# A two-layer encoder trunk on one core: work moved to GpSimd, and the first input ahead of the weights

## The chip, the cores and the metric

The kernel runs on one core of a Trainium2 chip. A core has five engines that run their own instruction streams and meet through semaphores: TensorE (PE in the profile; its weight loads are PEld), VectorE (DVE), ScalarE (ACT), GpSimd (POOL) and SyncE (SP), which here issues all DMAs. The metric is the device time of one execution in microseconds (us); three runs of the kernel before gave 2092.22, 2092.9 and 2097.98, a median of 2092.9.

## The reference

Two request groups, "prompt" (p, 1024 tokens) and "sample" (s, 512 tokens), go through the same two layers of width 1024. Cut to what matters:

```python
for l in range(2):
    z = rmsnorm(h, norm_g[l]) @ w_in[l]                 # 1024 -> 3328, split into 11 parts
    o = concat(hgrn2(...), rglru(...), diff_attn(...))  # three bidirectional branches, 1024 wide
    h = h + o @ w_out[l]
    h = h + sigmoid(h @ ple_gate_w[l]) * (p[l] @ ple_w[l])
y = rmsnorm(h, final_norm)
```

HGRN2 is a gated linear recurrence in chunks of 64, RG-LRU a convolution of width 4 with two scans per channel, and the attention subtracts two softmaxes. All of it is float32.

## The kernel before, in words

Activations lie transposed, 128 channels by 512 tokens in a tile, so the prompt has two token blocks and the sample one. Float32 products are made of three matmuls in a rounded format: every operand is split into a high part (ScalarE rounds it) and a low part (the value less its high part), and TensorE adds high·high, low·high and high·low. `load_split` (line 350) does this for a weight: one DMA of 256 KB into `wr`, a cast to `wh` on ScalarE (line 359) and a subtraction into `wl` on VectorE (line 360). `hilo` (line 326) does it for activations; `proj` (line 364) issues the three times four matmuls of each half of a weight column, 24 for a column of 1024 inputs.

A layer of a group has an input stage A (`phase_a`: projections by `w_in`, then attention, RG-LRU and HGRN2) and an output stage B (`phase_b`, one per token block). B multiplies by the eight columns of `w_out` (line 1067, each evacuated into `bh` on line 1073 and split again), then by the eight of `w_gate` (lines 1078 and 1087) and of the small `w_ple`. Three blocks in two layers make 48 columns of each, and 96 splits of `w_out` and 96 of `w_gate` weights.

The start is `first_norm` for the two prompt blocks: a DMA of each of the eight tiles `x`, a square on ScalarE (line 1135), and four matmuls by a column of ones that sum it (tile `ov`). Then `norm_in` (line 475) spreads 1/rms over the tile `rb`, and for each `x` VectorE multiplies by gain and `rb` (line 487) and `hilo` splits the product.

The order of all instructions is made ahead by a list scheduler in the kernel (`Recorder`). Each operation has a cost and a priority: its place in the program, plus `BIAS` of its stage, minus a share of the rank; offsets move loads forward (`WOFF`) or evacuations (`EVAC`, the lines inside `hp(EVAC)`). The scheduler keeps each engine's list in time by these costs and writes out one fixed sequence per engine. Stage names read A or B, the layer and the group: "A0s" is the sample's input stage in layer 0, with "at", "lru" or "hg" behind it for a branch. The prompt's stage B is woven into the sample's stage A, so that TensorE has matmuls while the branches run. Within an engine the sequence is strict: an instruction that waits holds all behind it.

Of the kernel before, what the change touches and what calls it, by code (L numbers as in the profile page):

```python
# [10 lines left out]
F32 = mybir.dt.float32  # L11
# [19 lines left out]
ORD_S = "aAbBhHlL"  # L31
BUFS = {"act": 32, "wr": 4, "wh": 5, "wl": 4, "pr": 1, "ph": 1, "pl": 1, "ev": 2, "io": 3, "acc": 1, "rb": 1, "tiny": 16, "sm": 4, "pre": 1, "lpr": 1,
        "m2x": 9, "m4x": 9, "m2y": 8, "m4y": 6}
WOFF, EVAC = 400, 900
RANK = 0.55
BIAS = {"A0sat": 400, "A1p": 100, "A1phg": 200, "A1plru": -50, "A1sat": -100, "A1shg": 50, "B0p0": -400, "B0p1": 300, "B0s0": -350, "B1p0": -50, "B1p1": 100, "B1s0": -200}
BANKS = {"pj": 3, "pt": 2, "ov": 1}
LANE = {
# [206 lines left out]
def tile_trunk(ctx: ExitStack, tc: tile.TileContext, a, groups, depth):  # L245
    nc = tc.nc
# [100 lines left out]
            V(8, lambda: nc.vector.scalar_tensor_tensor(out=t[:, c], in0=t[:, c], scalar=-0.5, in1=v[:, c], op0=MUL, op1=MUL), [t, v], [t])  # L347
            V(8, lambda s=s: nc.vector.scalar_tensor_tensor(out=dst[:, c], in0=t[:, c], scalar=1.5, in1=s(), op0=ADD, op1=MUL), [t, sk], [dst])

    def load_split(src, k, c=128, p="w", off=0):  # L350

        w = min(512, k * c)
        kk = w // c
        out = []
        for i in range(k // kk):
            raw, hi, lo = (T(p + x, [128, w], F32 if x == "r" else F32R, p + x) for x in "rhl")
            o = off - WOFF
            DMA(lambda raw=raw, i=i: nc.sync.dma_start(raw.t.rearrange("p (k c) -> p k c", k=kk), src[:, i * kk : i * kk + kk]), [], [raw], 512 * w, off=o, occ=0.4)
            A(w, lambda raw=raw, hi=hi: nc.scalar.copy(hi.t, raw.t), [raw], [hi], off=o)  # L359
            V(w, lambda raw=raw, hi=hi, lo=lo: nc.vector.tensor_tensor(out=lo.t, in0=raw.t, in1=hi.t.bitcast(F32), op=SUB), [raw, hi], [lo], off=o)  # L360
            out.append((hi, lo))
        return out

# [107 lines left out]
    def act(name="act"):  # L471
        return T("act", [128, 512], F32R, name)

    def norm_in(h_src, hkey, rs, gcol, gk, xs, hs=None):
        R.stage = f"norm{gk}"
        with hp(2000):
            pp = bcast_rs(rs, PT())
            pb = W5("rb", name="rb")
            A(512, lambda: nc.scalar.copy(pb.t, pp.t), [pp], [pb])
        for k in range(8):  # L480
            if hs is None:
                h = W5("io", name="nh")
                DMA(lambda h=h, k=k: nc.sync.dma_start(h.t, h_src(k)), [hkey(k)], [h], B2)
            else:
                h = hs[k]
            with hp(2000):
                V(512, lambda h=h, k=k: nc.vector.scalar_tensor_tensor(out=h.t, in0=h.t, scalar=gcol[:, k : k + 1], in1=pb.t, op0=MUL, op1=MUL), [h, pb, gk], [h], ps_=0.06)
                xh, xl = act(), act()
                hilo(h, xh, xl)
            xs[k] = (xh, xl)  # L490

    def head_tail(tg, ro, o, gcol, dk, sg_src, sgk, out_dst, outk, add=None):
# [551 lines left out]
    def phase_b(l, g, tb, n, oT, h_src, hk, hD):  # L1044
# [19 lines left out]
        h1D = dram.tile([8, 128, 512], F32, name=f"h1_{l}_{g}_{tb}")  # L1064
        hs = []
        for m in range(8):
            w = load_split(a["w_out"][l, m], 8)
            p = PJ()
            proj([p], w, [os_])
            h1 = W5("io", name="bh")  # L1070
            DMA(lambda h1=h1, m=m: nc.sync.dma_start(h1.t, h_src(m)), [hk(m)], [h1], B2)
            with hp(EVAC):
                V(512, lambda h1=h1, p=p: nc.vector.tensor_tensor(out=h1.t, in0=p.t, in1=h1.t, op=ADD), [p, h1], [h1])
                DMA(lambda h1=h1, m=m: nc.sync.dma_start(h1D[m], h1.t), [h1], [("h1", l, g, tb, m)], B2)
                xh, xl = act(), act()
                hilo(h1, xh, xl)
            hs.append((xh, xl))
        ahead = [load_split(a["w_gate"][l, m], 8) for m in range(2)]
        for k in range(2):
            xh, xl = act(), act()  # L1080
            r = W5("wr", name="p")
# [2 lines left out]
            ps_.append((xh, xl))  # L1084
        acc = W5("acc", name="acc")
        for m in range(8):
            w = ahead[m] if m < 2 else load_split(a["w_gate"][l, m], 8)
            wpl = load_split(a["w_ple"][l, m], 2, p="p")
            pg = PJ()
            proj([pg], w, [hs])  # L1090
            pp = PJ()
            proj([pp], wpl, [ps_])
            h1 = T("act", [128, 512], F32, "h2") if last else W5("io", name="bh1")
            fin.append(h1)
            DMA(lambda h1=h1, m=m: nc.sync.dma_start(h1.t, h1D[m]), [("h1", l, g, tb, m)], [h1], B2)
            with hp(EVAC):
                th = W5()
                A(512, lambda th=th, pg=pg: nc.scalar.activation(out=th.t, in_=pg.t, func=AF.Tanh, scale=0.5), [pg], [th])
                V(512, lambda th=th, pp=pp: nc.vector.scalar_tensor_tensor(out=th.t, in0=th.t, scalar=1.0, in1=pp.t, op0=ADD, op1=MUL), [th, pp], [th])
                V(512, lambda th=th, h1=h1: nc.vector.scalar_tensor_tensor(out=h1.t, in0=th.t, scalar=0.5, in1=h1.t, op0=MUL, op1=ADD), [th, h1], [h1])  # L1100
                if not last:
                    DMA(lambda h1=h1, m=m: nc.sync.dma_start(hD[m, :, sl], h1.t), [h1], [("h", l, g, tb, m)], B2)
                if m == 0:
                    A(512, lambda h1=h1: nc.scalar.activation(out=acc.t, in_=h1.t, func=AF.Square), [h1], [acc])
                else:
                    sq = W5()
                    A(512, lambda sq=sq, h1=h1: nc.scalar.activation(out=sq.t, in_=h1.t, func=AF.Square), [h1], [sq])
                    V(512, lambda sq=sq: nc.vector.tensor_tensor(out=acc.t, in0=acc.t, in1=sq.t, op=ADD), [acc, sq], [acc])
# [11 lines left out]
    rsd = {}  # L1120
    xs = {g: [[None] * 8 for _ in range(n // 512)] for g, n in groups}

    def first_norm(g, tb, tg="io", by_pe=True):

        hs = []
        rs = T("sm", [128, 4], F32, "rs")
        p = PT("ov") if by_pe else None
        acc = None if by_pe else W5("acc", name="acc")
        for k in range(8):
            x = W5(tg, name="x")  # L1130
            sq = acc if not by_pe and k == 0 else W5()
            DMA(lambda x=x, k=k: nc.sync.dma_start(x.t, a["x_" + g][k, :, blk(tb)]), [], [x], B2)
            hs.append(x)
            with hp(2000):
                A(512, lambda x=x, sq=sq: nc.scalar.activation(out=sq.t, in_=x.t, func=AF.Square), [x], [sq])

                def f(k=k, sq=sq):
                    for t in range(4):
                        mm(p[:, t : t + 1], sq[:, t * 128 : (t + 1) * 128], ones, k == 0 and t == 0, k == 7)

                if by_pe:
                    PE(0.9, f, [sq, "ones"], [p])
                elif k:
                    V(512, lambda sq=sq: nc.vector.tensor_tensor(out=acc.t, in0=acc.t, in1=sq.t, op=ADD), [acc, sq], [acc])
        if by_pe:
            with hp(2000):
                rsqrt(rs, lambda: p[:, 0:4], 4, 1.0 / 1024, EPS, srck=p)
        else:
            rs = stats_rs(acc)
        rsd[g, tb] = rs  # L1150
        return hs

    ng = [lay[l]["vec"][:, V_NG : V_NG + 8] for l in range(depth)]
    (g0, n0), rest = groups[0], groups[1:]
    x0 = first_norm(g0, 0, "m2x")
# [122 lines left out]
```

## Time and profile before

| | |
|---|---|
| median of three runs | 2092.9 us (2092.22 to 2097.98) |
| the profiled execution, its own time | 2098.01 us |
| its span, first to last instruction | 2096.2 us |
| TensorE busy | 1983.0 us, 95% |
| VectorE busy | 1535.0 us, 73% |
| ScalarE busy | 1214.7 us, 58% |
| GpSimd busy | 0.2 us, four memsets |
| granted clock of TensorE, mean | 0.975 |

Busy times are averages over stages with different limits, so they are read by stretch. A busy TensorE is not one at its peak, since the ends of matmuls are modelled; the count of matmuls in a stretch says more. "Idle before" in a row is what an engine waited before that row, with the releaser behind the arrow. PEclk is the granted clock: 1.00 is 2.4 GHz and 0.5 is 1.2 GHz. Layer 0 has its stage A of the prompt up to about 500 us, the sample's stage A with the prompt's stage B from there to about 900, and what is left of stage B up to 1050; layer 1 repeats it.

### The profile page before, as it was taken

The page shows a single profiled execution, that of the slowest core. Times are in us where ns is not written, and L with a number is a line of the kernel's source. Part 1 is how long each engine was busy: PE and PEld are TensorE (multiplying, and loading weights), DVE is VectorE, ACT ScalarE, POOL GpSimd, SP SyncE. Part 2 cuts the span into 40 slices and gives each one's busy share as a digit, 9 for nine tenths or more (in the row PEclk, how much of TensorE's full clock was granted, in tenths as well). Part 3 has the DMA queues.
Part 4 walks back from the last instruction along what each step waited for, and adds up shares of the span by engine and source line. Part 5 has one row for each costly group of instructions (what it writes and reads, how often), then busy time and mean ns, then how long its engine had stood idle before and what let it go on. Part 6 is the DMA issues. An engine that isn't in the chain of part 4 may idle for free.

```text
span 2096.2 us, 38258 instructions
## 1 busy us (share of the span) xinstructions
PE 1983.0 (95%) x14528; PEld 1613.2 (77%) x14528; DVE 1535.0 (73%) x2928; ACT 1214.7 (58%) x2053; POOL 0.2 (0%) x4
## 2 busy tenths in 40 slices
PE   7999889999999999899979988999999999889997
PEld 7887778887878787678767777888788878667875
DVE  5427678888988997754566767787789998785464
ACT  4338795766445468743438766676545654774332
POOL 0000000000000000000000000000000000000000
PEclk9999999999999999999989989999999999989998
DMA  4336433345444455564643462242464354547462
GB/s 154 109 98 195 164 109 110 111 147 167 152 152 149 150 179 186 179 204 161 197 158 127 150 183 86 91 123 85 150 213 146 123 171 158 179 143 258 126 205 89
DMA packets 187575, 316.53 MB, mean 151 GB/s; under 512 B 22016, under 2 KB 43008, under 8 KB 187392
## 3 DMA queue, kind: packets, MB, share of 16 engines
q1 hardware_dynamic: 187392, 314.09, 46.9%
q8 instruction: 115, 1.88, 0.4%
q14 instruction: 68, 0.56, 0.1%
HBM read 229.07 MB, written 84.93 MB: 150 GB/s over the span
## 4 chain that ended last, share of the span: by engine, by line
PE 70%; ACT 12%; DMA 7%; DVE 7%; issue 3%; SPq 0%; DVEq 0%; ACTq 0%
PE pj L316 52%; PE big L316 7%; PE ov L316 5%; PE pt L685 3%; DMA qk_p<-ev 3%; ACT ti L759 2%; ACT tr L759 1%; PE pt L316 1%; ACT T L761 1%; DMA qk_s<-ev 1%; ACT pp L670 1%; ACT tr L763 1%; ACT wh L359 1%; ACT L767 1%; DVE nm L667 1%
## 5 line engine op out<-in xcount | busy, mean ns | idle before, releaser
L316 PE MATMUL pj<-act,wh 128*128 128x512 f32 x3648 | 951.3, 399 | 16.9 <-ACT act L327 9.9
L316 PEld LDWEIGHTS pj<-act,wh 128*128 128x128 f32 x3648 | 683.5, 191 | 173.5 <-ACT act L327 13.9
L316 PE MATMUL pj<-act,wl 128*128 128x512 f32 x1824 | 496.4, 402 | 13.2 <-DVE wl L360 13.2
L316 PEld LDWEIGHTS pj<-act,wl 128*128 128x128 f32 x1824 | 344.3, 192 | 92.8 <-DVE wl L360 16.6
L360 DVE TENSOR_TENSOR wl<-wr,wh 128x512 fp32r<-128x512 f32 x400 | 272.6, 687 | 164.2 <-PE pj L316 111.7
L359 ACT CAST wh<-wr 128x512 fp32r<-128x512 f32 x400 | 243.4, 620 | 241.9 <-PE pj L316 163.7
L670 ACT ACTIVATE pp<-big,nm 128x1024 f32<-128x1024 f32 (+1 forms) x192 | 187.5, 977 | 92.1 <-DVE nm L667 74.4
L667 DVE TENSOR_REDUCE nm<-big 128x1 f32<-128x1024 f32 (+1 forms) x192 | 198.3, 1037 | 10.6 <-PE big L316 10.3
L316 PE MATMUL pj<-wh,act 128*128 128x256 f32 x768 | 146.3, 290 | 2.4 <-DVE ev L548 1.2
L316 PEld LDWEIGHTS pj<-wh,act 128*128 128x128 f32 x768 | 123.4, 194 | 9.3 <-issue 1.9
L316 PE MATMUL big<-ks,qs 96*128 96x512 f32 x320 | 113.5, 430 | 10.5 <-ACT pp L670 6.7
L688 ACT COPY wt<-pt 128x512 f32<-128x512 f32 x160 | 92.2, 588 | 44.1 <-PE pt L685 40.8
L316 PE MATMUL pj<-wl,act 128*128 128x256 f32 x384 | 109.3, 285 | 1.3 <-DVE wl L360 1.3
L677 DVE SCALAR_TENSOR_TENSOR pp<-pp,cc 128x1024 f32<-128x1024 f32 (+1 forms) x96 | 105.9, 1103 | 1.2
L685 PE MATMUL pt<-ident,pp 128*128 128x128 f32 x640 | 95.0, 278 | 2.2 <-DVE ev L591 0.7
L685 PEld LDWEIGHTS pt<-ident,pp 128*128 128x128 f32 x640 | 74.3, 141 | 22.9 <-issue 4.8
L316 PE MATMUL ov<-wt,dv 128*64 128x128 f32 x1280 | 82.2, 280 | 2.8 <-ACT wt L688 2.8
L316 PEld LDWEIGHTS ov<-wt,dv 128*64 128x64 f32 x1280 | 70.4, 139 | 17.0 <-issue 11.9
L759 ACT ACTIVATE tr<-big,der 64x512 f32<-64x512 f32 x96 | 65.4, 681 | 19.3 <-PE big L316 18.2
L316 PEld LDWEIGHTS pj<-wl,act 128*128 128x128 f32 x384 | 74.3, 194 | 1.5 <-DVE wl L360 1.5
L316 PE MATMUL pj<-act,ph 128*128 128x512 f32 x192 | 62.4, 406 | 11.1 <-ACT act L327 9.7
L316 PEld LDWEIGHTS big<-ks,qs 96*128 96x128 f32 x320 | 53.4, 191 | 24.1 <-ACT pp L670 12.3
(188 smaller groups left out, 2390.6 us busy)
## 6 DMA issues: line engine op xcount, KB each, us to landing
wr<-in_w_in SPq DMA_DIRECT2D x176, 256.0 KB
wr<-in_w_out SPq DMA_DIRECT2D x96, 256.0 KB
wr<-in_w_gate SPq DMA_DIRECT2D x96, 256.0 KB
h_p<-bh SPq DMA_DIRECT2D x48, 256.0 KB
sg_p<-ev SPq DMA_DIRECT2D x32, 256.0 KB
wr<-in_w_v SPq DMA_DIRECT2D x32, 256.0 KB
qk_p<-ev SPq DMA_DIRECT2D x32, 256.0 KB
act<-oT_p SPq DMA_DIRECT2D x32, 256.0 KB
```

Of the source, the lines that this page charges most:

```text
L316: nc.tensor.matmul(out, lhsT, rhs, start=start, stop=stop, skip_group_check=True)
L359: A(w, lambda raw=raw, hi=hi: nc.scalar.copy(hi.t, raw.t), [raw], [hi], off=o)
L360: V(w, lambda raw=raw, hi=hi, lo=lo: nc.vector.tensor_tensor(out=lo.t, in0=raw.t, in1=hi.t.bitcast(F32), op=SUB), [raw, hi], [lo], off=o)
L667: V(n, lambda nm=nm, pv=pv: nc.vector.tensor_reduce(out=nm.t, in_=pv(), axis=mybir.AxisListType.X, op=ALU.max, negate=True), [b], [nm])
L670: A(n, lambda p=p, pv=pv, nm=nm, s1=s1, s2=s2, j=j, qt=qt, H=H: nc.scalar.activation(out=p.t, in_=pv(), func=AF.Exp, bias=nm.t, accum_out= ...
L677: V(n, lambda P=P, c=c: nc.vector.scalar_tensor_tensor(out=P[0].t, in0=P[1].t, scalar=c.t, in1=P[0].t, op0=MUL, op1=ADD), [P[0], P[1], c], ...
L685: nc.tensor.transpose(pt[:, kt * 128 : kt * 128 + 128], P[0][:, c0 : c0 + 128], ident)
L688: A(512, lambda wt=wt, pt=pt, kb=kb: nc.scalar.copy(wt[:, blk(kb)], pt.t), [pt], [(wt, kb)])
L759: A(512, lambda dst=dst, pg=pg, r=r, dr=dr, hb=hb, col=col, h=h, o=o: nc.scalar.activation(out=dst[h, dr, :], in_=pg[o, r, :], func=AF.Tan ...
L761: A(512, lambda T2=T2, tr=tr, dr=dr, col=col: nc.scalar.activation(out=T2[:, dr, :], in_=tr[:, dr, :], func=AF.Tanh, scale=d["n2"][:, col] ...
L763: A(512, lambda tr=tr, dr=dr, col=col: nc.scalar.activation(out=tr[:, dr, :], in_=tr[:, dr, :], func=AF.Exp, scale=d["n4"][:, col], bias=d ...
L767: A(1024, lambda T2=T2: nc.scalar.activation(out=T2.t, in_=T2.t, func=AF.Sqrt, scale=-0.25), [(T2, 0), (T2, 1)], [(T2, 0), (T2, 1)], tab=" ...
```

## The change

The low parts of the `w_out` and `w_gate` weights go from VectorE to GpSimd (192 subtractions). In the two first norms, every other tile is multiplied by `rb` on GpSimd; the gain then comes in as the scale of ScalarE's cast and as the scalar of VectorE's subtraction, so that VectorE has one operation for such a tile and not two. The loads of the first eight `x` tiles get an offset of -1500. `EVAC` and seven entries of `BIAS` change, of which two are new.

```diff
-WOFF, EVAC = 400, 900
+WOFF, EVAC = 400, 1100
-BIAS = {"A0sat": 400, "A1p": 100, ... "A1sat": -100, ... "B0p0": -400, ... "B0s0": -350, "B1p0": -50, ... "B1s0": -200}
+BIAS = {"A0sat": 400, "A0shg": -50, ... "A1sat": -150, "A1slru": 200, "B0p0": -200, ... "B0s0": -550, "B1p0": -100, ... "B1s0": -300}
-    def load_split(src, k, c=128, p="w", off=0):
+    def load_split(src, k, c=128, p="w", off=0, pool=False):
...
+            if pool:
+                R("POOL", 1.1, lambda raw=raw, hi=hi, lo=lo: nc.gpsimd.tensor_tensor(out=lo.t, in0=raw.t, in1=hi.t.bitcast(F32), op=SUB), [raw, hi], [lo], lat=1.3, off=o)
+            else:
+                V(w, lambda raw=raw, hi=hi, lo=lo: nc.vector.tensor_tensor(out=lo.t, in0=raw.t, in1=hi.t.bitcast(F32), op=SUB), [raw, hi], [lo], off=o)
...
+                if hs is not None and k % 2:
+                    R("POOL", 1.1, lambda h=h: nc.gpsimd.tensor_tensor(out=h.t, in0=h.t, in1=pb.t, op=MUL), [h, pb], [h], lat=1.3)
+                    A(512, lambda h=h, xh=xh, k=k: nc.scalar.activation(out=xh.t, in_=h.t, func=AF.Copy, scale=gcol[:, k : k + 1]), [h, gk], [xh])
+                    V(512, lambda h=h, xh=xh, xl=xl, k=k: nc.vector.scalar_tensor_tensor(out=xl.t, in0=h.t, scalar=gcol[:, k : k + 1], in1=xh.t.bitcast(F32), op0=MUL, op1=SUB), [h, xh, gk], [xl], ps_=0.06)
+                else:
+                    V(512, lambda h=h, k=k: nc.vector.scalar_tensor_tensor(out=h.t, in0=h.t, scalar=gcol[:, k : k + 1], in1=pb.t, op0=MUL, op1=MUL), [h, pb, gk], [h], ps_=0.06)
+                    hilo(h, xh, xl)
...
-            w = load_split(a["w_out"][l, m], 8)
+            w = load_split(a["w_out"][l, m], 8, pool=True)
...
-        ahead = [load_split(a["w_gate"][l, m], 8) for m in range(2)]
+        ahead = [load_split(a["w_gate"][l, m], 8, pool=True) for m in range(2)]
...
-            w = ahead[m] if m < 2 else load_split(a["w_gate"][l, m], 8)
+            w = ahead[m] if m < 2 else load_split(a["w_gate"][l, m], 8, pool=True)
...
-    def first_norm(g, tb, tg="io", by_pe=True):
+    def first_norm(g, tb, tg="io", by_pe=True, off=0):
...
-            DMA(lambda x=x, k=k: nc.sync.dma_start(x.t, a["x_" + g][k, :, blk(tb)]), [], [x], B2)
+            DMA(lambda x=x, k=k: nc.sync.dma_start(x.t, a["x_" + g][k, :, blk(tb)]), [], [x], B2, off=off)
...
-    x0 = first_norm(g0, 0, "m2x")
+    x0 = first_norm(g0, 0, "m2x", off=-1500)
```

The start of the program on SyncE's queue, before: `wr` are weights of the first projection, `x` the input, `ident` and `masks` constants.

```order
L324 DMA vec_69<-in_vecs 128x198
L358 DMA wr<-in_w_in 128x512 x4
L1132 DMA x<-in_x_p 128x512 x8
L1156 DMA ident<-in_c_ident 128x128
L1132 DMA x<-in_x_p 128x512 x5
L358 DMA wr<-in_w_in 128x512
```

The same place now:

```order
L324 DMA vec_69<-in_vecs 128x198
L1140 DMA x<-in_x_p 128x512 x8
L358 DMA wr<-in_w_in 128x512 x4
L1164 DMA ident<-in_c_ident 128x128
L1140 DMA x<-in_x_p 128x512 x8
L1170 DMA masks<-in_c_masks 128x384
```

The first eight `x` tiles stand ahead of the four weight loads, and the second eight in one piece behind them.

VectorE at the first norm, before: line 487 multiplies `x` by gain and `rb`, line 328 makes the low part.

```order
L487 SCALAR_TENSOR_TENSOR x<-x,vec_69,rb 128x512 x3
L328 TENSOR_TENSOR act<-x,act 128x512
L487 SCALAR_TENSOR_TENSOR x<-x,vec_69,rb 128x512
L328 TENSOR_TENSOR act<-x,act 128x512
L487 SCALAR_TENSOR_TENSOR x<-x,vec_69,rb 128x512
L328 TENSOR_TENSOR act<-x,act 128x512 x2
```

The same place now, with the multiplication on line 496 and the low part of an odd tile on line 494 (its product with `rb` stands in GpSimd's list):

```order
L496 SCALAR_TENSOR_TENSOR x<-x,vec_69,rb 128x512 x3
L328 TENSOR_TENSOR act<-x,act 128x512
L496 SCALAR_TENSOR_TENSOR x<-x,vec_69,rb 128x512
L494 SCALAR_TENSOR_TENSOR act<-x,vec_69,act 128x512
L363 TENSOR_TENSOR pl<-pr,ph 128x256
L328 TENSOR_TENSOR act<-x,act 128x512
```

VectorE has 12 operations on the eight tiles where it had 16.

VectorE in the sample's RG-LRU of layer 0, before, between two of its four channel tiles (`u` the convolution, `ti` and `T` its gates, `ul` the low part of `u`, `s` its result; `wl`, `bh` and `act` belong to the prompt's stage B):

```order
L739 SCALAR_TENSOR_TENSOR u<-zp,vec_69,u 128x512
L360 TENSOR_TENSOR wl<-wr,wh 128x512
L739 SCALAR_TENSOR_TENSOR u<-zp,vec_69,u 128x512
L360 TENSOR_TENSOR wl<-wr,wh 128x512 x2
L773 SCALAR_TENSOR_TENSOR ti<-ti,u 128x1024
L328 TENSOR_TENSOR ul<-u,uh 128x512
```

The same place now:

```order
L804 SCALAR_TENSOR_TENSOR s<-s,sg 128x512
L747 SCALAR_TENSOR_TENSOR u<-zp,vec_69,u 128x512
L1116 TENSOR_TENSOR acc<-acc,ev 128x512
L747 SCALAR_TENSOR_TENSOR u<-zp,vec_69,u 128x512
L363 TENSOR_TENSOR pl<-pr,ph 128x256
L747 SCALAR_TENSOR_TENSOR u<-zp,vec_69,u 128x512
```

The low parts of stage B's weights are gone from between the steps of `u`. In TensorE's list 33 of the layer's 96 such low parts are now used ahead of the sample's last RG-LRU matmul of layer 0, and 32 of 96 in layer 1.

## Rows read from the trace of the kernel before

**Rows 1.** The page's head and its busy time by engine.

```profile
span 2096.2 us, 38258 instructions
PE 1983.0 (95%) x14528; PEld 1613.2 (77%) x14528; DVE 1535.0 (73%) x2928; ACT 1214.7 (58%) x2053; POOL 0.2 (0%) x4
```

**Rows 2.** Windows: busy us of each engine (instructions) in six stretches.

```profile
core 0: us, PE busy (x) PEld busy (x) DVE busy (x) ACT busy (x) POOL busy (x), PEclk, DMA share, GB/s
200.00:350.00 150.00, 137.49 (x876) 115.06 (x876) 105.36 (x151) 116.83 (x179) 0.00 (x0) 0.97 0.44 139
500.00:650.00 150.00, 150.00 (x2131) 123.64 (x2131) 132.98 (x304) 76.61 (x140) 0.00 (x0) 1.00 0.45 142
650.00:800.00 150.00, 149.66 (x1507) 118.89 (x1508) 137.57 (x335) 86.57 (x172) 0.00 (x0) 1.00 0.56 177
800.00:900.00 100.00, 86.00 (x369) 64.49 (x367) 77.05 (x121) 82.81 (x124) 0.00 (x0) 0.95 0.56 184
900.00:1050.00 150.00, 148.71 (x656) 121.34 (x656) 79.51 (x138) 55.89 (x102) 0.00 (x0) 1.00 0.56 180
1775.00:1900.00 125.00, 110.24 (x465) 85.39 (x464) 96.82 (x154) 91.62 (x145) 0.00 (x0) 0.93 0.54 182
```

**Rows 3.** Timeline of the first 60 us: start, length, engine, line, operation, [idle before].

```profile
0.24 0.10 POOL L1269 MEMSET const-float32-0.0<- 128x1 f32 x1 [0.24 <-issue]
...
0.80 0.06 DVE L323 MEMSET ones<- 128x1 f32 x1 [0.80 <-PEq L1269]
...
3.95 0.62 ACT L359 CAST wh<-wr 128x512 fp32r<-128x512 f32 x1 [0.45 <-DMA wr<-in_w_in]
...
8.52 0.63 ACT L1135 ACTIVATE ev<-x 128x512 f32<-128x512 f32 x1 [0.33 <-DMA x<-in_x_p]
...
9.20 18.93 PE L316 MATMUL ov<-ones,ev 128*128 128x1 f32 x88 [9.20 <-DVE pre L425]
...
11.15 0.63 ACT L1135 ACTIVATE ev<-x 128x512 f32<-128x512 f32 x1 [1.15 <-PE ov L316]
...
29.84 8.53 PE L316 MATMUL ov<-ones,ev 128*128 128x1 f32 x40
...
38.23 2.05 PE L316 MATMUL pj<-act,wh 128*128 128x512 f32 x4
...
44.52 1.08 PE L316 MATMUL pj<-act,wl 128*128 128x512 f32 x4
...
47.43 0.59 ACT L479 COPY rb<-pt 128x512 f32<-128x512 f32 x1 [0.25 <-PE pt L316]
...
52.03 0.62 ACT L327 CAST act<-x 128x512 fp32r<-128x512 f32 x1 [1.25 <-DVE x L487]
...
52.70 2.50 PE L316 MATMUL pj<-act,wh 128*128 128x512 f32 x5 [1.07 <-ACT act L327]
```

**Rows 4.** Groups by form, whole run, VectorE: two 128x512 forms with two inputs.

```profile
L781 DVE TENSOR_TENSOR_SCAN ti<-tr,ti 128x512 f32<-128x512 f32 x24 | 29.8, 1240 | 0.2
...
L328 DVE TENSOR_TENSOR act<-x,act 128x512 fp32r<-128x512 f32 x16 | 10.9, 689 | 0.9 <-ACT act L327 0.7
```

**Rows 5.** Groups by form, VectorE, 650 to 860 us: the weights' low parts.

```profile
L360 DVE TENSOR_TENSOR wl<-wr,wh 128x512 fp32r<-128x512 f32 x43 | 29.4, 687 | 3.8 <-ACT o L500 1.3 <-ACT KT L886 1.0 <-PE pj L316 0.9
```

**Rows 6.** Waits of TensorE, 800 to 900 us: total us, times, longest.

```profile
PE pj L316 <- DVE wl L360: 5.7, 3, 4.3
PE pj L316 <- ACT act L327: 2.6, 1, 2.6
...
PE big L316 <- DVE gwl L722: 1.5, 1, 1.5
PE big L316 <- DVE ul L328: 1.1, 1, 1.1
```

**Rows 7.** Waits of TensorE, 1775 to 1900 us.

```profile
PE pj L316 <- ACT act L327: 6.8, 2, 5.2
PE pj L316 <- DVE wl L360: 3.8, 1, 3.8
```

More of the change, by code (lines that the diff above doesn't have):

```diff
@@ L33 @@
         "m2x": 9, "m4x": 9, "m2y": 8, "m4y": 6}
-WOFF, EVAC = 400, 900
+WOFF, EVAC = 400, 1100
 RANK = 0.55
-BIAS = {"A0sat": 400, "A1p": 100, "A1phg": 200, "A1plru": -50, "A1sat": -100, "A1shg": 50, "B0p0": -400, "B0p1": 300, "B0s0": -350, "B1p0": -50, "B1p1": 100, "B1s0": -200}
+BIAS = {"A0sat": 400, "A0shg": -50, "A1p": 100, "A1phg": 200, "A1plru": -50, "A1sat": -150, "A1slru": 200, "B0p0": -200, "B0p1": 300, "B0s0": -550, "B1p0": -100, "B1p1": 100, "B1s0": -300}
 BANKS = {"pj": 3, "pt": 2, "ov": 1}
@@ L359, in load_split @@
             A(w, lambda raw=raw, hi=hi: nc.scalar.copy(hi.t, raw.t), [raw], [hi], off=o)
-            V(w, lambda raw=raw, hi=hi, lo=lo: nc.vector.tensor_tensor(out=lo.t, in0=raw.t, in1=hi.t.bitcast(F32), op=SUB), [raw, hi], [lo], off=o)
+            if pool:
+                R("POOL", 1.1, lambda raw=raw, hi=hi, lo=lo: nc.gpsimd.tensor_tensor(out=lo.t, in0=raw.t, in1=hi.t.bitcast(F32), op=SUB), [raw, hi], [lo], lat=1.3, off=o)
+            else:
+                V(w, lambda raw=raw, hi=hi, lo=lo: nc.vector.tensor_tensor(out=lo.t, in0=raw.t, in1=hi.t.bitcast(F32), op=SUB), [raw, hi], [lo], off=o)
             out.append((hi, lo))
@@ L485, in norm_in @@
                 h = hs[k]
+            xh, xl = act(), act()
             with hp(2000):
-                V(512, lambda h=h, k=k: nc.vector.scalar_tensor_tensor(out=h.t, in0=h.t, scalar=gcol[:, k : k + 1], in1=pb.t, op0=MUL, op1=MUL), [h, pb, gk], [h], ps_=0.06)
-                xh, xl = act(), act()
-                hilo(h, xh, xl)
+                if hs is not None and k % 2:
[5 more added lines that the diff above has]
+                    hilo(h, xh, xl)
             xs[k] = (xh, xl)
```

## The prediction

> **What bounds the kernel now.** I read the page's busy times first: TensorE 95%, VectorE 73%, ScalarE 58%, GpSimd nothing [rows 1]. So TensorE sets the time, and only stretches in which it stands or runs slowly have something to give. The windows find them [rows 2]. From 500 to 800 us TensorE is full (150.00 and 149.66 of 150) although VectorE is busy for 132.98 and 137.57: relief of VectorE alone buys nothing there as long as TensorE has matmuls. From 900 to 1050, pure output stage, 656 matmuls take 148.71 us, 0.227 us each, and VectorE is at 79.51 of 150: again nothing. Time is lost from 800 to 900 (14.0 us idle, clock 0.95) and from 1775 to 1900 (14.8 us idle, clock 0.93), where the sample's RG-LRU meets the output stages. A mean clock of 0.95 over 100 us is 10 us at 1.2 GHz and 5.0 us of lost work; 0.93 over 125 us is 17.5 us and 8.8 us of lost work. The waits view says what TensorE stood for, and most of it hangs on VectorE's list [rows 6, 7]. The start is read from the timeline: TensorE's first instruction comes at 9.20 us and it works without a break of note until the second norm [rows 3].
>
> **The start.** The first weight's cast starts at 3.95 us, when its 256 KB have landed; the first square waits for the first `x`, of the same size but behind four weights, until 8.52 [rows 3]. With `x` in front the square starts at 3.95 and TensorE 0.68 later, at 4.63 where it was 9.20: -4.6 us. After that the sums set the pace: 88 instructions in 18.93 us, eight to a tile, 1.72 us a tile, with ScalarE waiting for TensorE between squares (1.15 us) [rows 3]. So later landings are hidden. What moves back are four weight loads, their casts (0.62 each, inside ScalarE's waits of 1.15) and their low parts; the first projection that needs them starts at 38.23, or 33.7 after the change, and they land about 8 us in, as the `x` did.
>
> One doubt is TensorE's clock. Four matmuls take 2.05 us at 38.23 and 1.08 at 44.52 [rows 3], so the engine runs at half rate through the sums and rises in between. If it rises at the same instant as before, matmuls made in the 4.6 us gained go at half rate and 2.3 us remain. It has matmuls without a break from its first instruction on, and now starts earlier, so I take 4.6 and keep 2.3 as an end.
>
> The second norm holds TensorE too: `rb` at 47.43, the cast of the fourth tile at 52.03 behind VectorE, matmuls at 52.70 [rows 3]. Odd tiles are now the product of GpSimd. No row has such an operation. From below it costs 0.69 us, VectorE's time for the same shape [rows 4]; from above I let it reach 2.7 us, half of the 24 matmuls (24 x 0.227 = 5.4) beside which two are needed. The nearest pair of rows is a memset of 128x1, 0.10 us on GpSimd and 0.06 on VectorE [rows 3]; 0.69 times 1.7 is 1.15 us, and I take that, close to VectorE's slowest two-input row of this shape (1.24) [rows 4]. (GPSIMD Engine Reference in the Trainium skill, section on performance versus the Vector engine, has 4497 ns for 2048 columns; a quarter, 1.12 us, would be its estimate, and no run here shows it.) The fourth tile is GpSimd's second: 48.0 + 2 x 1.15 = 50.3, its cast done 0.6 later at 50.9 where it was 52.65: -1.7 us. At 2.7 us it would be 1.4 late instead. VectorE has one operation for each odd tile and not two, so 8 of some 0.69 us [rows 4] go. ScalarE's casts wait for GpSimd here, with only the casts of later tiles behind them; that is in the sum. Start: -4.6 - 1.7 = -6.3 us, between -0.9 (the clock's doubt and 2.7 us) and -7.2 (0.69 us).
>
> **The weights' low parts.** 192 subtractions of 0.687 us leave VectorE, 132 us, and GpSimd gets 192 x 1.15 = 221 us. In the pure output stages, with 33 and 32 used earlier, 127 lie: GpSimd needs 2.3 us for each 5.4 us of matmuls, VectorE was half idle, and the effect is nothing. Buffers hold two columns (four `wl`), so 0.5 us more of delay is covered by a column's 5.4; without that cover each late pair would cost its 0.9.
>
> In the two RG-LRU stretches the effect is real. Before, 43 low parts stood in VectorE's list from 650 to 860 us, 29.4 us of it [rows 5]. Of the 14.0 us idle from 800 to 900, TensorE waited 5.7 for `wl`, 1.5 for `gwl`, 1.1 for `ul`, and 2.6 for a cast that itself waits for VectorE's evacuation [rows 6]. I count the first three and half the fourth, 9.6 us, or 0.69 of the idle time, and the same share of the clock's 5.0: -13.0 us. From 1775 to 1900 only the 3.8 for `wl` [rows 7], 0.26 of the idle time, with that share of 8.8: -6.1 us. What is late next is ScalarE, busy 82.81 of 100 and 91.62 of 125 [rows 2], so the rest I leave. -19.1 us, between 0 and the whole of both stretches, 14.0 + 5.0 + 14.8 + 8.8 = -42.6.
>
> What comes back is what GpSimd takes from VectorE when both read. No row shows it: between 0 and 65 x 1.15 = 75 us of VectorE standing. VectorE is occupied 77% of the stretch, so most of these operations meet one of its own; standing half of each time would undo the whole relief (65 x 0.58 = 38 against 65 x 0.69 = 45). I take +8, a bit under half of the gain.
>
> **The order.** `EVAC` and `BIAS` rearrange the fill of TensorE; its matmuls stay the same in number. From 200 to 350 us, where the lists first differ, it is idle 12.5 us [rows 2]; a better or worse weave there moves some of that either way. I take 0 and keep 8 at either side.
>
> **The sum** against the profiled execution: 2098.0 - 6.3 - 19.1 + 8 = 2080.6 us. It was 5.1 us above the median of the runs, so the forecast is 2075.5, said as 2076. A measurement of this kernel tells 0.3%, 6.3 us, from no change: faster is below 2086.6, slower above 2099.2.
>
> **The rivals.**
> *GpSimd and VectorE block each other.* Place: 650 to 860 us and 1710 to 1862 us, where the prompt's output stage is woven into the sample's input stage. For it: VectorE is busy 137.57 of 150 there [rows 2], TensorE's list now reckons with a VectorE that is free of these 65 operations, and it is strict, so a late VectorE stops it at once. If each of the 65 stops VectorE for its full 1.15 us, that is 75 us in place of 45 removed, +30 us; the start still gives 6.3: 2093 + 30 - 6 = 2117 us. It decides from 0.78 us a piece on ((45 + 6.3) / 65). Against it: the low parts come two to a column of 5.4 us, so that GpSimd is at rest more than half of the time, and TensorE has fill to go on with. SBUF — State Buffer in the Trainium skill, section "Who interferes with whom", has it as a rule: a VectorE instruction with two SBUF inputs and a GpSimd instruction that reads SBUF exclude each other for the whole instruction. By that rule the +8 would be some 19 and the forecast 2087. No row of before can show it, since GpSimd does nothing there.
> *The relief is hidden anyway.* ScalarE's activations pace the RG-LRU, or the blocking just eats the relief. Then only the start is left: 2093 - 6 = 2087, or 2089 with the smaller start. For it: ScalarE's 83% from 800 to 900 [rows 2].
> *Both stretches close.* With VectorE out of the way and the fill placed better, idle time and clock come back whole: 2093 - 6 - 43 = 2044, say up to 2055 with the usual remainder. Against it: ScalarE again.
> *GpSimd is the bound.* Above 2.7 us an operation, it would pace the pure stages: at 3.2 us 127 / 2 x 1.0 = +64 us, 2151. For it only that no row shows the operation.
>
> **How the numbers follow.** Forecast (2058 to 2086) 0.56; both stretches close 0.08; hidden 0.18; blocking 0.15; GpSimd the bound 0.03. Faster is the first two and nothing else, 0.64; same 0.18; slower 0.18. The likeliest one's own range is 2058 to 2086. For 8 in 10, I leave out half of the closing case below and the worse half of blocking and the bound above: 2052 to 2108.
>
> **What would show it.** Right: the first sum of squares at about 4.6 us; the second norm's block of matmuls some 6 us earlier; GpSimd's rows at 1.1 to 1.3 us; idle time from TensorE to `wl` gone at the end of the sample's RG-LRU of both layers, and the clock there nearer to 1.00. Wrong: VectorE's two-input 128x512 rows longer than 0.69 us in the mean beside GpSimd's, above all between 650 and 860; GpSimd's rows over 2 us; or the idle time simply found again under another releaser, ScalarE's `act` or `tr`. If the start gains 2 us and not 4.6, the clock was the doubt that counted.

## The result and the profile after

The changed kernel takes 2123.02 us (median of four runs, 2113.55 to 2126.43); the kernel before, run beside it, 2095.39 us. The ratio is 1.0118, 95% interval 1.0095 to 1.0141: slower, where 2076 us and faster had been forecast, and outside the range of 2052 to 2108.

The page's head after the change, answering to [rows 1]:

```profile
span 2124.6 us, 38518 instructions
PE 1987.3 (94%) x14528; PEld 1613.4 (76%) x14528; DVE 1512.0 (71%) x2728; ACT 1213.3 (57%) x2053; POOL 287.2 (14%) x204
```

VectorE has 200 instructions fewer (2728 for 2928). At 0.69 us each that is some 137 us of work, yet its busy time falls by only 23 us (1535.0 to 1512.0). The instructions that are left must have become longer. The groups by form show which; first the kernel before, VectorE, whole run (count, then busy us and mean ns of one, then idle time before):

```profile
L328 DVE TENSOR_TENSOR act<-bh,act 128x512 fp32r<-128x512 f32 x48 | 33.0, 688 | 9.8 <-ACT act L327 9.4
L1073 DVE TENSOR_TENSOR bh<-pj,bh 128x512 f32<-128x512 f32 x48 | 33.0, 687 | 22.7 <-PE pj L316 22.4
L1108 DVE TENSOR_TENSOR acc<-acc,ev 128x512 f32<-128x512 f32 x42 | 28.9, 688 | 14.1 <-ACT ev L1107 14.1
L360 DVE TENSOR_TENSOR pl<-pr,ph 128x256 fp32r<-128x256 f32 x48 | 20.3, 422 | 15.2 <-ACT ph L359 15.0
```

The same forms after the change, and the two that answer to [rows 4]:

```profile
L328 DVE TENSOR_TENSOR act<-bh,act 128x512 fp32r<-128x512 f32 x48 | 42.2, 879 | 19.6 <-ACT act L327 19.2
L1116 DVE TENSOR_TENSOR acc<-acc,ev 128x512 f32<-128x512 f32 x42 | 41.4, 986 | 21.7 <-ACT ev L1115 21.7
L1081 DVE TENSOR_TENSOR bh<-pj,bh 128x512 f32<-128x512 f32 x48 | 32.9, 686 | 74.1 <-PE pj L316 68.3 <-DMA bh<-h_s 3.8 <-DMA bh<-h_p 1.3
L789 DVE TENSOR_TENSOR_SCAN ti<-tr,ti 128x512 f32<-128x512 f32 x24 | 31.8, 1325 | 0.2
L363 DVE TENSOR_TENSOR pl<-pr,ph 128x256 fp32r<-128x256 f32 x48 | 26.9, 559 | 22.2 <-ACT ph L359 21.7
L328 DVE TENSOR_TENSOR act<-x,act 128x512 fp32r<-128x512 f32 x8 | 7.6, 948 | 0.0
```

GpSimd's two groups in the same view:

```profile
L361 POOL TENSOR_TENSOR wl<-wr,wh 128x512 fp32r<-128x512 f32 x192 | 274.4, 1434 | 1768.7 <-ACT wh L359 874.2 <-DVE cc L683 617.1 <-PE pj L316 208.3
L492 POOL TENSOR_TENSOR x<-x,rb 128x512 f32<-128x512 f32 x8 | 12.6, 1608 | 37.1 <-ACT rb L482 37.1
```

The VectorE forms here that read two tiles in SBUF are longer: 688 became 879, 688 became 986, 422 became 559. The form that reads the accumulator `pj` in PSUM and one tile in SBUF is not (687 and 686). It stands in the same list, so it is no general slowness of VectorE. ScalarE is not slower either: it is busy for 1213.3 us, where it was 1214.7 [rows 1]. Single instructions show what happens. Timeline of VectorE and GpSimd in the output stage that runs alone (start, length):

```profile
943.12 1.29 POOL L361 TENSOR_TENSOR wl<-wr,wh 128x512 fp32r<-128x512 f32 x1 [1.56 <-ACT wh L359]
943.24 1.72 DVE L1108 SCALAR_TENSOR_TENSOR bh<-ev,bh 128x512 f32<-128x512 f32 x1
...
945.71 1.30 POOL L361 TENSOR_TENSOR wl<-wr,wh 128x512 fp32r<-128x512 f32 x1 [1.30 <-ACT ev L1115]
945.72 1.83 DVE L1116 TENSOR_TENSOR acc<-acc,ev 128x512 f32<-128x512 f32 x1 [0.76 <-ACT ev L1115]
```

GpSimd ends at 944.41 and VectorE at 944.96; GpSimd at 947.01 and VectorE at 947.55. VectorE comes 0.12 and 0.01 us after GpSimd, and each time it is done about 0.55 us after GpSimd is. That fits a VectorE that does its work only when GpSimd's instruction is over.

Where the time went is in the windows of after, answering to [rows 2] (busy us of each engine and instructions, then granted clock, DMA share, GB/s):

```profile
core 0: us, PE busy (x) PEld busy (x) DVE busy (x) ACT busy (x) POOL busy (x), PEclk, DMA share, GB/s
650.00:800.00 150.00, 134.39 (x1402) 104.00 (x1397) 129.93 (x277) 88.71 (x162) 39.44 (x26) 0.95 0.47 151
800.00:900.00 100.00, 87.34 (x379) 69.49 (x379) 75.90 (x96) 64.46 (x105) 37.76 (x25) 0.93 0.56 184
...
1775.00:1900.00 125.00, 103.39 (x495) 79.65 (x494) 85.72 (x137) 80.52 (x129) 38.49 (x27) 0.93 0.48 154
```

TensorE was full from 650 to 800 us, 149.66 of 150, and now has 134.39 and a clock of 0.95: GpSimd's first low part comes in this stretch, at 667.19 us. From 800 to 900 and from 1775 to 1900, the two stretches that were to close, it has 87.34 for 86.00 and 103.39 for 110.24. These windows lie at fixed times while the work in them has moved (465 matmuls before and 495 now in the last), so they show that the stretches did not close and not what each lost; that is read below from a run in the same order. The waits that had been there [rows 6, 7] went and others came; TensorE from 800 to 900 and then from 1775 to 1900:

```profile
PE ov L316 <- DVE acc L1116: 9.4, 1, 9.4
PE big L316 <- DVE ul L328: 2.5, 1, 2.5
```

```profile
PE ov L316 <- DVE acc L1116: 9.4, 1, 9.4
PE pj L316 <- ACT act L327: 6.3, 1, 6.3
```

The waits for `wl` (5.7 and 3.8 us) are gone, as forecast. In their place TensorE waits 9.4 us, twice, for the sum of squares `acc`. This is one of the forms that GpSimd stops, but most of the wait is not GpSimd's. The same two waits, in a run below that keeps this order and leaves GpSimd's low parts out:

```profile
830.88 1.87 PE L316 MATMUL ov<-ones,acc 128*128 128x1 f32 x8 [5.94 <-DVE acc L1120]
...
1859.17 1.87 PE L316 MATMUL ov<-ones,acc 128*128 128x1 f32 x8 [8.91 <-DVE acc L1120]
```

So 3.4 and 0.5 us of them come with GpSimd's low parts, and the rest is there in this order without them.

The start, in the timeline after, answering to [rows 3]:

```profile
3.94 0.63 ACT L1143 ACTIVATE ev<-x 128x512 f32<-128x512 f32 x1 [0.49 <-DMA x<-in_x_p]
...
4.62 18.93 PE L316 MATMUL ov<-ones,ev 128*128 128x1 f32 x88 [4.62 <-ACT ev L1143]
...
33.66 2.05 PE L316 MATMUL pj<-act,wh 128*128 128x512 f32 x4
...
40.24 1.09 PE L316 MATMUL pj<-act,wl 128*128 128x512 f32 x4
...
48.02 3.12 PE L316 MATMUL pj<-act,wh 128*128 128x512 f32 x6 [0.26 <-ACT act L327]
```

The first sum came at 4.62 for 9.20, as forecast (4.63). The rise of the rate moved along (four matmuls take 2.05 us at 33.66 and 1.09 at 40.24), so the doubt about the clock did not count. What makes the early matmuls slow stays open: the granted clock is 1.00 (2.4 GHz) from 33 to 39.5 us, and before it was 1.00 from 38 to 44 us. The block behind the second norm moved from 52.70 to 48.02. That row has one matmul more than the old one; the same five start at 48.64, so the block came 4.1 and not 6.3 us earlier.

### The profile page after: what moved, and what is told of

Its sections match the earlier page's. It is cut to its first block, busy times and chain, and to the rows that moved or that the text cites. A ratio compares the mean times of both kernels' runs of the same rounds, so it can differ in the third digit from the quotient of the medians.

```text
span 2124.6 us, 38518 instructions
## 1 busy us (share of the span) xinstructions
PE 1987.3 (94%) x14528; PEld 1613.4 (76%) x14528; DVE 1512.0 (71%) x2728; ACT 1213.3 (57%) x2053; POOL 287.2 (14%) x204
## 5 line engine op out<-in xcount | busy, mean ns | idle before, releaser
L361 POOL TENSOR_TENSOR wl<-wr,wh 128x512 fp32r<-128x512 f32 x192 | 274.4, 1434 | 1768.7 <-ACT wh L359 874.2
L363 DVE TENSOR_TENSOR wl<-wr,wh 128x512 fp32r<-128x512 f32 x208 | 141.2, 685 | 93.2 <-PE pj L316 67.5
L1107 DVE SCALAR_TENSOR_TENSOR ev<-ev,pj 128x512 f32<-128x512 f32 x48 | 32.8, 683 | 75.4 <-ACT ev L1106 60.8
L1081 DVE TENSOR_TENSOR bh<-pj,bh 128x512 f32<-128x512 f32 x48 | 32.9, 686 | 74.1 <-PE pj L316 68.3
```

The source lines that it names most:

```text
L361: R("POOL", 1.1, lambda raw=raw, hi=hi, lo=lo: nc.gpsimd.tensor_tensor(out=lo.t, in0=raw.t, in1=hi.t.bitcast(F32), op=SUB), [raw, hi], [lo ...
```

## The experiments

Three theories after the result: A, GpSimd's reads stop VectorE's instructions with two inputs in SBUF; B, the new `BIAS` and `EVAC` make a worse order; C, GpSimd makes the low parts too late. Each ratio below is against the kernel before on the same chip, with its 95% interval.

**The weights back on VectorE**, everything else of the change kept.

```diff
-            w = load_split(a["w_out"][l, m], 8, pool=True)
+            w = load_split(a["w_out"][l, m], 8)
...   # and both w_gate calls
```

> The changed kernel with the low parts of the output stages' weights back on VectorE; the first norms, the early input, EVAC and BIAS stay, and the list is planned anew. Theory A (while GpSimd reads two inputs, VectorE's instructions with two inputs in SBUF stand, and its strict list makes TensorE wait): the loss is gone, 2080 to 2098 us, and act<-bh and acc on VectorE are back from 879 and 986 ns to 0.69 us. Theory B (the new EVAC and BIAS give a worse order, GpSimd is harmless): it stays at 2110 to 2125 us. Theory C (GpSimd's low parts come too late, 1.43 us in place of 0.69): as A in the total.

The kernel before had 2096.34 us here. This one: 2089.27 us, ratio 0.9965 (0.9954 to 0.9976); the two-input forms are back at 687 and 688 ns. The whole loss hangs on the weights' low parts, and the rest of the change is a small gain.

**The old table** in the changed kernel.

```diff
-WOFF, EVAC = 400, 1100
+WOFF, EVAC = 400, 900
...   # and BIAS of before
```

> The changed kernel with EVAC and BIAS of the kernel before; GpSimd keeps its 200 operations. A: still slow, 2105 to 2130 us, with VectorE's two-input forms near 0.9 us. B: the loss is gone, 2080 to 2092 us. C: still slow, 2105 to 2130 us, but with TensorE's waits on wl at its head.

2158.07 us, 1.0293 (1.0269 to 1.0318), beyond everything expected. B falls, and the opposite holds: with the low parts on GpSimd, the new table takes back 35 us.

**GpSimd writes and hardly reads.** In the changed kernel's order it reads one column of the weight and writes zeros over the rest three times, which leaves the low parts out of the products.

```diff
-    nc.gpsimd.tensor_tensor(out=lo.t, in0=raw.t, in1=hi.t.bitcast(F32), op=SUB)
+    nc.gpsimd.tensor_tensor(out=lo[:, 0:1], in0=raw[:, 0:1], in1=hi[:, 0:1].bitcast(F32), op=SUB)
+    for _ in range(3):
+        nc.gpsimd.memset(lo[:, 1:w].bitcast(F32), 0.0)
...   # both in one operation of the list, of the same cost
```

> The changed kernel, in which GpSimd reads one column of each weight tile and writes zeros over the rest three times, so that the low parts are left out of the products; plan, order and waits are the same, and I expect 1.3 to 1.6 us a tile. A: VectorE's two-input forms are back at 0.69 us except in the first norms, and the time falls to 2070 to 2092 us. B and C: it stays at 2110 to 2125 us, since order and GpSimd's length are as they were.

2087.89 us, 0.9963 (0.9946 to 0.9979). GpSimd and VectorE by form:

```profile
L364 POOL MEMSET wl<- 128x511 f32 x576 | 303.1, 526 | 22.1
L362 POOL TENSOR_TENSOR wl<-wr,wh 128x1 fp32r<-128x1 f32 x192 | 55.7, 290 | 1643.7 <-ACT wh L359 848.2 <-DVE cc L688 619.4 <-issue 116.6
```

```profile
L328 DVE TENSOR_TENSOR act<-bh,act 128x512 fp32r<-128x512 f32 x48 | 33.1, 689 | 20.1 <-ACT act L327 19.8
L1121 DVE TENSOR_TENSOR acc<-acc,ev 128x512 f32<-128x512 f32 x42 | 29.0, 689 | 23.5 <-ACT ev L1120 23.3
```

A tile costs GpSimd 290 + 3 x 526 = 1.87 us, longer than the subtraction's 1.43, and nothing is lost: C falls, A stands. The changed kernel is 35 us slower than this one (2123.0 against 2087.9).

**GpSimd reads beside the kernel before.** In before's order it repeats each of the 192 subtractions, in four pieces, into a tile that nobody uses.

```diff
+    for c in range(0, w, 128):
+        nc.gpsimd.tensor_tensor(out=spare, in0=raw[:, c : c + 128], in1=hi[:, c : c + 128].bitcast(F32), op=SUB)
...   # behind VectorE's own subtraction, for w_out and w_gate
```

> The kernel before with its order untouched; behind each of VectorE's 192 low parts of w_out and w_gate, GpSimd makes the same subtraction once more in four pieces into a spare tile that nobody reads. A: VectorE's act<-bh and acc rise from 0.69 to 0.85 us or more, its busy time by 60 us or more, and the kernel takes 2110 to 2140 us. B and C: nobody waits for GpSimd and the order is the old one, 2090 to 2100 us.

2153.34 us, 1.0265 (1.0243 to 1.0287). VectorE by form:

```profile
L329 DVE TENSOR_TENSOR act<-bh,act 128x512 fp32r<-128x512 f32 x48 | 39.4, 822 | 8.5 <-ACT act L328 8.1
L1080 DVE TENSOR_TENSOR bh<-pj,bh 128x512 f32<-128x512 f32 x48 | 32.9, 684 | 22.2 <-PE pj L317 22.1
```

A again, and more than expected: GpSimd's pieces take four times 661 ns, 508 us in all, and the weights' buffers wait for them as well: SyncE's queue stands 208.8 us for GpSimd before it loads a weight. Its control:

**GpSimd writes beside the kernel before**, with a read of one column.

```diff
+    nc.gpsimd.tensor_tensor(out=spare[:, 0:1], in0=raw[:, 0:1], in1=hi[:, 0:1].bitcast(F32), op=SUB)
+    for _ in range(6):
+        nc.gpsimd.memset(spare[:, 1:128], 0.0)
...   # behind VectorE's own subtraction, for w_out and w_gate
```

> The kernel before, in its own order; beside each of the 192 low parts that VectorE makes, GpSimd reads one column and then writes six pieces of 128 columns into a tile that nobody reads, work that the reference does not need. It is the control to the run in which GpSimd read both inputs: the buffers wait for GpSimd's one-column read here too. Theory A: VectorE's forms stay at 686 to 690 ns and the time within 5 us of before, 2092 to 2100 us. Rival (GpSimd being busy, or holding the weights' buffers, costs the 58 us): 2120 us or more.

2096.43 us, 1.0015 (1.0002 to 1.0029); the same two forms are at 688, with GpSimd busy for 303.7 us. So VectorE's forms grow with the reading in this order too. The 57 us of time are not the reading's alone: here SyncE's queue stands only 32.1 us for GpSimd, and what the longer hold of the buffers cost in the run before is not shown. Nor do these runs part reading from the kind of operation, as what only wrote was always a memset.

**The start alone**: the first input ahead of the weights, nothing else.

```diff
-    x0 = first_norm(g0, 0, "m2x")
+    x0 = first_norm(g0, 0, "m2x", off=-1500)
```

> The kernel before with the fetch of the first input ahead of the weights and nothing else of the change. Theory D (what is won at the start is kept to the end): the first PE sums come 4.6 us sooner, as they did in the changed kernel, and nothing later takes it back: ratio 0.9978, some 2091 us. Rival (a later wait takes it up, since the weights now land later): ratio 0.999 to 1.001, 2094 to 2098 us.

2091.49 us, 0.9983 (0.9972 to 0.9993): -3.6 us of 4.6, with the interval holding all of it.

**The start with the norms on GpSimd.**

```diff
+                if hs is not None and k % 2:
+                    R("POOL", 1.1, lambda h=h: nc.gpsimd.tensor_tensor(out=h.t, in0=h.t, in1=pb.t, op=MUL), [h, pb], [h], lat=1.3)
...   # and the rest of the change's edit of norm_in
```

> As the run with the input first, and every other tile of the first norms is multiplied on GpSimd; the weights' low parts stay on VectorE and the order's table is that of before. Theory A (GpSimd's reads stop VectorE): the four multiplies VectorE keeps in the second norm are lengthened by what it is spared, so PE's block after that norm starts at 48.0 us with or without GpSimd: within 1 us of the run with the input first, 2091 us. Rival (the prediction's term of 1.7 us): 2089 us or less. If the blocked norms cost more than they spare: 2092 to 2094 us.

2093.00 us, 0.9978 (0.9965 to 0.9991): no different from the run with the input first. The second norm without and then with GpSimd:

```profile
43.17 2.08 DVE L487 SCALAR_TENSOR_TENSOR x<-x,vec,rb 128x512 f32<-128x512 f32 x3 [1.30 <-ACT rb L479]
```

```profile
42.86 5.21 DVE L493 SCALAR_TENSOR_TENSOR x<-x,vec,rb 128x512 f32<-128x512 f32 x3 [0.17 <-ACT rb L479]
42.91 6.30 POOL L489 TENSOR_TENSOR x<-x,rb 128x512 f32<-128x512 f32 x4 [10.39 <-ACT rb L479]
```

Three multiplications take 5.21 us in place of 2.08, beside four of GpSimd that take 6.30, as if the two engines took turns. What VectorE is spared it stands.

**The new table with everything on VectorE** and the input first.

```diff
-WOFF, EVAC = 400, 900
+WOFF, EVAC = 400, 1100
...   # and BIAS of the change
```

> The input first and the changed kernel's order table, with all of the weights' low parts and all norms on VectorE. Theory: the table by itself, without GpSimd's work, is worth between 0 and 3 us against the run with the input first, and the norms on GpSimd nothing, so this stands where the changed kernel with its weights back on VectorE stood, 2086 to 2092 us. Rival (the table only fits a GpSimd that takes the low parts, and costs without them): 2095 us or more.

2089.14 us, 0.9966 (0.9952 to 0.9981): 2.4 us below the run with the input first, not told apart from it, and level with the run that put the weights back. These two beat both kernels, by some 7 us the one before and 34 the changed one.

**No low parts at all.** The 192 instructions are dropped, PE multiplies by zeros, and the scheduler plans without them.

```diff
-                R("POOL", 1.1, lambda ...: nc.gpsimd.tensor_tensor(out=lo.t, ...), [raw, hi], [lo], lat=1.3, off=o)
+                lo = zero
...   # and the tile of zeros in the matmuls
```

> The changed kernel with the low parts of the output stages' weights made by nobody: PE multiplies by one tile of zeros in their place (this leaves out that part of the computation), so VectorE is spared all 192 instructions, about 132 us of its time, and GpSimd does nothing for it. Theory R0 (VectorE's relief is hidden, the matrix products set the time): within 4 us of the changed kernel with its weights back on VectorE, 2085 to 2093 us. Rival R1 (the prediction's term: the two RG-LRU stretches close by 19 us): 2070 us or less. In between, 2071 to 2084 us: a part of the relief is real.

2100.59 us, 1.0019 (1.0009 to 1.0030): with less to do it is slower than any version with all of it on VectorE. The plan is another one: from 1845 to 1890 us TensorE waits 14.0 us in one piece for the cast of the next output stage's inputs:

```profile
PE pj L316 <- ACT act L331: 16.8, 2, 14.0
```

As a test of the relief it is spoilt by its order, so three more runs kept an order to the instruction.

**The 192 instructions not issued**, in the order of the version with the weights on VectorE (the planner still reckons with them).

```diff
+                V(w, lambda lo=lo: lo.t, [raw, hi], [lo], off=o)   # planned, issues nothing
+                lo = (lo, zero)
...   # and the tile of zeros in the matmuls
```

> The changed kernel with its weights back on VectorE, in that kernel's order to the instruction, but the 192 low-part instructions of the output stages are not issued and PE multiplies by a tile of zeros in their place (this leaves out that part of the computation). It shows what sparing VectorE 132 us is worth where neither GpSimd nor a new order comes in. Theory R0 (the matrix products set the time and the relief is hidden): within 4 us of the kernel with the weights on VectorE (2089 us), 2085 to 2093 us. Rival R1 (the prediction's term of 19 us): 2070 us or less. In between, 2071 to 2084 us: part of the relief is real, and the run without low parts lost it to its new order.

2088.82 us, 0.9965 (0.9953 to 0.9978), against 2089.27 with the instructions. VectorE is at 1423.8 us for 1536.4, and the relief is worth nothing that these intervals could tell.

**The same in the changed kernel's order.**

```diff
+                R("POOL", 1.1, lambda lo=lo: lo.t, [raw, hi], [lo], lat=1.3, off=o)   # planned, issues nothing
+                lo = (lo, zero)
...   # and the tile of zeros in the matmuls
```

> The changed kernel in its own order to the instruction, but GpSimd's 192 low-part instructions are not issued and PE multiplies by a tile of zeros (this leaves out that part of the computation). Theory A (GpSimd's reads stop VectorE, and that is all of the loss): the lengthened forms are back at 686 to 690 ns and the time at that of the kernel in which GpSimd only wrote, 2080 to 2090 us. Rival (the changed order is worse by itself, or waits for other things): 2100 us or more.

2088.91 us, 0.9966 (0.9954 to 0.9978). Its VectorE, with the same 2728 instructions as the changed kernel's, is the cleanest price of the blocking:

```profile
PE 1977.9 (95%) x14528; PEld 1609.2 (77%) x14528; DVE 1422.3 (68%) x2728; ACT 1213.0 (58%) x2053; POOL 13.0 (1%) x13
```

1512.0 - 1422.3 = 89.7 us of VectorE standing, and 2123.0 - 2088.9 = 34 us of time. ScalarE is the same, 1213.3 and 1213.0.

Where this fell can be read between the same instructions of the two runs: from 650 us to the sum of the prompt's first block, from there to the end of layer 0, and from 1700 us to that sum in layer 1. First the changed kernel, then this run:

```profile
650.00:850.41 200.41, 172.15 (x1560) 132.82 (x1554) 170.17 (x326) 125.70 (x220) 55.00 (x36) 0.94 0.48 155
850.41:1068.50 218.09, 210.02 (x909) 170.31 (x909) 110.95 (x153) 91.28 (x159) 83.75 (x60) 0.97 0.58 186
1700.00:1894.33 194.33, 168.90 (x1436) 130.94 (x1434) 147.74 (x264) 113.54 (x185) 51.62 (x36) 0.97 0.48 156
```

```profile
649.30:830.88 181.58, 167.68 (x1561) 131.00 (x1555) 145.98 (x326) 125.53 (x220) 0.00 (x0) 0.96 0.54 170
830.88:1047.10 216.22, 208.84 (x908) 168.47 (x908) 85.87 (x153) 91.82 (x159) 0.00 (x0) 0.98 0.58 188
1675.20:1859.17 183.97, 167.40 (x1437) 131.30 (x1435) 126.09 (x264) 113.01 (x185) 0.00 (x0) 0.97 0.51 167
```

In the two stretches with the sample's RG-LRU, 72 of GpSimd's instructions make VectorE 24.2 and 21.6 us longer, and the stretches are 18.8 and 10.4 us longer. In the pure output stages the other 120 make it longer by as much, 25.1 us in layer 0 and 19.0 in layer 1 (118.6 for 99.6), and these are only 1.9 and 1.5 us longer. Another 3.4 of the 36.7 us between the two spans come from 1068.5 to 1700 us, where GpSimd does nothing in either run; their cause is open. TensorE's extra waits in the changed kernel are many small ones: for `acc` 27.8 us in place of 23.8 over the run, for RG-LRU's `uh` and `ul` 17.8 in place of 10.3, for the attention's `pp` 9.6 in place of 5.2. It is also busy for 9.4 us more (1987.3 against 1977.9), at a mean clock of 0.970 in place of 0.974.

**GpSimd in four of six output stages**, without the first prompt block of each layer.

```diff
-            w = load_split(a["w_out"][l, m], 8, pool=True)
+            w = load_split(a["w_out"][l, m], 8, pool=(g, tb) != ("p", 0))
...   # and both w_gate calls
```

> The changed kernel with GpSimd taking the low parts in only four of the six output stages, 128 of 192 instructions: those of the first prompt block of each layer, beside which the sample's RG-LRU runs, go back to VectorE. Theory P (blocking costs where PE waits for VectorE and nothing elsewhere, the prediction's zero for the stages that run alone): 2087 to 2097 us. Rival Q (the loss goes with the number of GpSimd's instructions, two thirds of 34 us): some 2112 us, over 2105 us.

2100.30 us, 1.0015 (1.0000 to 1.0029): 11 us above the version without GpSimd's low parts. Neither theory: 128 of the 192 instructions go with a third of the loss. The list was planned anew here, and its order differs from the other version's from 813 us on, so the 11 us are not shown to be GpSimd's alone. The window from 800 to 900 us, in the version with the weights on VectorE and then in this one:

```profile
800.00:900.00 100.00, 85.27 (x362) 67.84 (x361) 70.59 (x111) 66.16 (x103) 0.00 (x0) 0.90 0.56 187
```

```profile
800.00:900.00 100.00, 80.03 (x340) 62.82 (x339) 68.51 (x83) 64.80 (x100) 36.28 (x23) 0.90 0.54 176
```

GpSimd's low parts begin here, and TensorE gets 22 matmuls fewer done. From the first block's sum (`acc`) to the last block's, where the output stages run alone, it is 232.5 us in this run and 227.9 in the other in layer 0, and 218.6 and 216.5 in layer 1.

**The relief in the order of before.**

```diff
+                V(w, lambda lo=lo: lo.t, [raw, hi], [lo], off=o)   # planned, issues nothing
+                lo = (lo, zero)
...   # and the tile of zeros in the matmuls
```

> The kernel before in its own order to the instruction, but the 192 low-part instructions of the output stages are not issued and PE multiplies by a tile of zeros in their place (this leaves out that part of the computation). It is the prediction's relief by itself, in the order from whose rows the 19.1 us were worked out. Theory R0 (hidden in this order too: PE's waits for low parts pass to the waits next to them): 2090 to 2096 us. Rival R1 (the prediction's term holds in this order, and the new order had already taken it): 2080 us or less. In between, 2081 to 2089 us: a third to three quarters of the term.

2090.93 us, 0.9980 (0.9966 to 0.9994): -4.3 us (-7.1 to -1.3), inside the 2090 to 2096 of the theory that it is hidden here too, though the interval leaves out zero. TensorE's waits from 800 to 900 us in it:

```profile
PE pj L316 <- ACT wh L362: 7.5, 3, 4.8
```

Before, it was 5.7 for `wl` [rows 6], and for `wh`, ScalarE's cast of the same weight, this:

```profile
PE pj L316 <- ACT wh L359: 2.2, 2, 1.3
```

Together that was 7.9 us, and now it is 7.5 for `wh` alone: the low part had been the last of a pair whose other half ends almost as late.

## Why the prediction was wrong

**The step that failed first** is "I take +8, a bit under half of the gain". It sized the blocking as a part of the relief, and not by what VectorE would stand. In the two stretches it was meant for, VectorE stood 45.8 us behind 72 instructions of GpSimd, 0.64 us each, and the two took 29 us longer, where 8 had been allowed; over the whole kernel it is 89.7 us of standing and 34.1 of time (2123.0 - 2088.9). The prediction had the better size beside it: standing half of each time was 65 x 0.58 = 38 us (which is not the whole of the 45 that it is said to undo). Against the blocking it set that GpSimd is at rest more than half of the time and that TensorE has fill to go on with. Neither kept VectorE from meeting GpSimd, and beside the RG-LRU only some 17 of the 46 us stayed hidden. In the pure output stages nearly all did: 44 us stood, 3.4 lost, so the zero put there was right but for these. The rule of the Trainium skill (SBUF — State Buffer, section "Who interferes with whom"), by which a VectorE instruction with two SBUF inputs and a GpSimd instruction that reads SBUF exclude each other, was quoted, priced at 19 us in place of 8, and then not used for the forecast. The trace agrees with it in each part: 688 to 879 ns with two SBUF inputs, 687 to 686 with one in PSUM, 689 when GpSimd writes and reads one column.

**The relief of 19.1 us** was hidden as well. In the order of before it is 4.3 us, in the new order nothing (2088.82 against 2089.27). "What is late next is ScalarE ... so the rest I leave" was the right engine and the wrong size: it kept 0.69 of the idle time as VectorE's, and the wait passed to the `wh` of the same weight. Reading a wait's releaser says who came last, not by how much. So a change without any blocking would have come to some 2089 us, the figure of the rival "hidden anyway", and with the blocking to 2123, near the 2117 of the rival in which the engines block each other. That rival had its place right: 29 of the 36.7 us between the two spans lie in its two stretches. Its sum was not, and that it came near is luck: it took 75 us of standing less 45 of relief, where 46 us stood, at 29 us of time, and the relief gave nothing.

**The start** was right for the input (-4.6 in the trace, 0.9983 in time) and wrong for the norm's 1.7 us. It is the same blocking: 1.61 us an instruction on GpSimd for the 1.15 priced, and 1.74 for 0.69 on VectorE.

**GpSimd's price** of 1.15 us for a low part was low: 1.43 in the mean. The rival in which GpSimd is the bound is out; it is 14% busy.

**The order** was put at 0 with 8 to either side. With everything on VectorE it is -2.4 us, inside that. With GpSimd's low parts the same table is worth 35 us: moving them costs 67 us under the old table (2158.1 against 2091.5 with the input first) and 34 under the new.

The account: 2095.4 before, -3.6 for the input, 0 for the norms, -2.4 for the table, 0 for the relief and +34.1 for the blocking make 2123.5 us; 2123.0 were measured. Each term is a difference of two medians or a ratio that is known to some 2 us to either side, so part of so close a sum is luck.

## What to carry to other kernels

Before work is moved from one engine to another, ask what the two share: here GpSimd's reading stops VectorE's two-input instructions, so that of 113 us taken off VectorE (1535.0 to 1422.3) 90 came back. What that costs depends on the stretch: 3.4 of 44 us in the pure output stages, where VectorE is busy for half of the time, and 29 of 46 beside the RG-LRU, where it is busy for 318 of 395 us. A wait that names an engine is worth only the distance to the next releaser, which an order kept to the instruction with the work left out measures in one run. And an order tuned with a change in place has to be tried without it: here the new table hid half of the price of moving the low parts.

## What the runs showed that was not expected

A GpSimd instruction stops even small VectorE instructions with a single input in SBUF. VectorE and GpSimd in the changed kernel where layer 0's second prompt block ends (start, length):

```profile
1013.12 2.54 POOL L361 TENSOR_TENSOR wl<-wr,wh 128x512 fp32r<-128x512 f32 x2 [7.55 <-ACT wh L359]
1013.19 0.15 DVE L338 TENSOR_SCALAR rv<-ov 128x4 f32<-128x4 f32 x1
1013.38 1.06 DVE L341 TENSOR_SCALAR ry<-rv 128x4 int32<-128x4 int32 x1
1014.48 1.20 DVE L342 TENSOR_SCALAR ry<-ry 128x4 int32<-128x4 int32 x1
1015.71 0.17 DVE L346 TENSOR_TENSOR rt<-ry 128x4 f32<-128x4 f32 x1
```

`ov` is in PSUM, and that instruction takes its 0.15 us. The two behind it take 1.06 and 1.20 us, where the means before were 0.166 and 0.164 (nine each), and end when GpSimd's two end. They stand on the path from a block's sum to its norm. (The section of the Trainium skill named above puts `tensor_scalar` in its two-port mode under the same lock; these two rows agree, though none shows which mode they ran in.)
